# Moving every activation tile of a streamed fp32 matmul chain to one fixed byte distance from the weight tiles

## The chip, the cores and the metric

The kernel runs on one core of one Trainium2 chip. The metric is the device time of one execution in microseconds (us), taken as the median of several executions. Five engines matter: TensorE (PE in the profile, with its weight loads shown apart as PEld), VectorE (DVE), ScalarE (ACT), GpSimd (POOL), and SyncE (SP), which issues all DMAs.

## The reference

Two layers of a decoder trunk on 256 positions of width 1024, batch 1, all in fp32. Layer 0 mixes tokens by dilated window attention, layer 1 by an mLSTM block; each layer then has a squared-ReLU MLP and a gated embedding.

```
for i in range(2):
    if i == 0:
        x = x + dilated_attention(rms_norm(x, a_norm), a_w_qkv, ..., a_w_o)
    else:
        x = x + mlstm_mixer(rms_norm(x, b_norm), b_w_up, ..., b_w_down)
    x = x + squared_relu_mlp(rms_norm(x, mlp_norm[i]), mlp_w1[i], mlp_w2[i])   # 1024 -> 4096 -> 1024
    gate = sigmoid(rms_norm(x, ple_norm[i]) @ ple_w_gate[i])
    x = x + gate * (p[i] @ ple_w_proj[i])
```

Nearly all the arithmetic is in products of 256 positions with large weight matrices: `a_w_qkv` (1024 x 9216), `a_w_o`, `b_w_up` (1024 x 4096), `b_w_down` (2048 x 1024), two pairs `mlp_w1`, `mlp_w2` and two `ple_w_gate`.

## The kernel before

**The weight stream.** All weights lie in DRAM as one sequence of units of 128 partitions x 2048 fp32 (1 MB), in the order of use: `qkv`, `proj0`, `woA`, `woB`, `w1_0`, `w2_0`, `gate0`, `xm`, `z0` to `z3`, `wd0`, `proj1`, `wd1`, `w1_1`, `w2_1`, `gate1`. SyncE fetches a unit four units ahead into one of three `raw` buffers. `split` (lines 180 and 181) turns 512 columns at a time into a rounded part `hi` (ACT) and a remainder `lo` (DVE), both of type fp32r, in 12 rotating buffers each. Each buffer is 2048 bytes long in a partition, so all of them start at the same byte modulo 256.

**The matmuls.** Activations are held the same way, as a pair of high and low part. `stream` (lines 335 to 337) does three matmuls for each 128 x 128 weight tile and adds them up in PSUM:

```
mm(acc[:, q], wh, h, start=first, stop=False, ...)   # L335
mm(acc[:, q], wh, l, start=False, stop=False, ...)   # L336
mm(acc[:, q], wl, h, start=False, stop=last, ...)    # L337
```

Here the weight tile (512 bytes of a partition's row) is the stationary operand and is loaded anew for each matmul; the activations (256 columns, 1024 bytes) are the moving one. In `qkv_block` (lines 503 to 505) it is the other way round: the activations are stationary and 512 columns of weights move.

**Which activations meet the weights.** `hh`/`hl` (the pair `hA`): `qkv`, `w1_0`, `xm`, `z0` to `z3`, `wd1`, `gate1`. `oTh`/`oTl`: `woA`, `woB`. `hidh`/`hidl`: `w2_0`, `w2_1`. `hGh`/`hGl`: `gate0`. `hBh`/`hBl`: `wd0`, `w1_1`. `pT`: `proj0`, `proj1`. `hWh`/`hWl`: two of the 18 blocks of `qkv`.

**What sets the order.** Work is counted in slots of four weight tiles. `at(slot, f)` hangs small pieces of work on a slot, and they are written out when the slot closes, so they stand between stream matmuls on TensorE. Ahead of each `w1`, `gate` and `xm` stretch, `rstd_rows` does so twice: `st.total` (line 276, four short matmuls in the trace) two slots in, and `spread` (line 297, four more) six slots in. In the mLSTM part (`xm` to `wd0`) many more pieces stand between them.

**Where tiles lie.** Pools take SBUF from the low end in the order in which they are opened (or from the high end, with `side="right"`), and tiles follow each other within a pool, so every size moves what comes behind it. Two tiles that nobody uses, `gap0` and `gap1` of 64 bytes, stand ahead of and behind the pools of `hi` and `lo`.

Of the kernel before, what the change touches and what calls it, by code (L numbers as in the profile page):

```python
# [10 lines left out]
F32 = mybir.dt.float32  # L11
F32R = mybir.dt.float32r
I32 = mybir.dt.int32
AF = mybir.ActivationFunctionType
# [4 lines left out]
D, S, P = 1024, 256, 128  # L19
# [113 lines left out]
def build(tc, a):  # L133
    nc = tc.nc
    ctx = ExitStack()
    with ctx:
        _build(ctx, tc, nc, a)


def _build(ctx, tc, nc, a):  # L140
    def pool(n, b=1, c=ctx, **k):
        if "space" not in k:
            k["reuse_waits"] = "tile"
        return c.enter_context(tc.tile_pool(name=n, bufs=b, **k))

    base = pool("base")
# [1 line left out]

    pool("gap0").tile([P, 16], F32, name="gap0")
    hip, lop = pool("hi", 3 * UC // HU), pool("lo", 3 * UC // HU)  # L150
    pool("gap1").tile([P, 16], F32, name="gap1")
    psa = pool("psa", 3, space=PSUM)
    pst = pool("pst", 2, space=PSUM)
    pss = pool("pss", 2, space=PSUM)
# [3 lines left out]
    act = nc.scalar.activation  # L158
# [67 lines left out]


    xctx0 = ExitStack()
    x = pool("x0", c=xctx0, side="right").tile([P, KT, S], F32, name="x")
    prm = base.tile([P, NP], F32, name="prm")  # L230
    ident = base.tile([P, P], F32, name="ident")
    ones = base.tile([P, P], F32, name="ones")
# [6 lines left out]
                nc.sync.dma_start(x[:, 2 * j:2 * j + 2], a["x"][:, 2 * j:2 * j + 2])  # L239
            nc.sync.dma_start(raw[u][:, j * 512:(j + 1) * 512], a["w"][u, :, j * 512:(j + 1) * 512])  # L240
    nc.sync.dma_start(ident, a["eye"])
    first = base.tile([P, 1], F32, name="first")
    act(first, ones[:, 0:1], AF.Exp)

    warm = psm.tile([P, 512], F32, name="sm")
    for _ in range(WARM):
# [5 lines left out]

    hA = [base.tile([P, KT, S], F32R, name=f"h{n}") for n in "hl"]
    sqp = pool("sq", 2)

    class Stats:

# [25 lines left out]
    def rsqrt(y, v, shape):  # L283
        t = sqp.tile(shape, F32, name="rt")
        dve.tensor_scalar(y.bitcast(I32), v.bitcast(I32), -0.5, RSQRT_MAGIC, op0=ALU.mult, op1=ALU.add)
        for _ in range(3):
            dve.tensor_tensor(t, y, y, op=ALU.mult)
            dve.scalar_tensor_tensor(t, t, -0.5, v, op0=ALU.mult, op1=ALU.mult)
            dve.scalar_tensor_tensor(y, t, 1.5, y, op0=ALU.add, op1=ALU.mult)
# [62 lines left out]
    atp = pool("attn", c=actx)  # L352
# [24 lines left out]

    def first_stats():
        st.total()
        sw = atp.tile([P, P], F32, name="sw")  # L380
        dve.tensor_copy(sw[:, 0:64], st.s[:, 192:256])
        dve.tensor_copy(sw[:, 64:128], st.s[:, 0:64])
        for n, t in ((2, st.s[:, 64:192]), (3, sw)):
            mm(st.ps[:, 256 + n:257 + n], t, ones[:, 0:1], start=True, stop=True)
        v = atp.tile([P, 4], F32, name="v4")
        dve.tensor_scalar(v, st.ps[:, 256:260], 1.0 / D, EPS, op0=ALU.mult, op1=ALU.add)
        dve.tensor_scalar(epsx, v[:, 0:2], EPS, None, op0=ALU.mult)
        rsqrt(rx, v, [P, 4])

    def wrap():  # L390
        for n in range(2):
            act(hW[n][:, :, 0:64], hA[n][:, :, 192:256], AF.Copy)
            act(hW[n][:, :, 64:128], hA[n][:, :, 0:64], AF.Copy)

    at(0, first_stats)
    at(8, wrap)

# [281 lines left out]

    mctx = ExitStack()  # L680
    mp = pool("mlp0", c=mctx)
    hid = [mp.tile([P, 32, S], F32R, name=f"hid{n}") for n in "hl"]
    hgp = pool("hG", c=xctx0, side="right")
    hG = [hgp.tile([P, KT, S], F32R, name=f"hG{n}") for n in "hl"]
# [4 lines left out]

    xp1 = pool("x1")  # L690
    xn = xp1.tile([P, KT, S], F32, name="xn")
    hB = [xp1.tile([P, KT, S], F32R, name=f"hB{n}") for n in "hl"]
    mctx = ExitStack()
    mp = pool("gate0", c=mctx)
# [18 lines left out]
    lp = pool("lstm", c=lctx)  # L713
# [123 lines left out]
    def gates_c():  # L837
        ps = SMALL["ps"]
        for b in range(2):
            nc.tensor.transpose(ps[0:4, 16 + b * P:16 + (b + 1) * P], ai[:, b], ident)  # L840
        arow = lp.tile([4, S], F32, name="arow")
        dve.tensor_copy(arow, ps[0:4, 16:16 + S])
        dve.tensor_tensor_scan(Mrow, arow, arow, -3e38, ALU.max, ALU.max)

# [12 lines left out]
    zp = None  # L857
# [94 lines left out]
    for part, _ in CORE:  # L952
        if part == "z0":
            z_units(0, lp)
            while fill:
                for f, args in fill.pop(min(fill)):
                    f(*args)
            close_x()
            t = clock[0]
            for n, f in zip(GT, (gates_b, gates_c, gates_d)):  # L960
                at(t + n, f)
            for h in range(4):
                for n, f in zip(HO, (decay, memory, factor, merge)):
                    at(t + HS[h] + n, f, h)
        elif part[0] == "z":
            z_units(int(part[1]), zp)
        elif part == "proj1":
            prep, ph = proj(1, zp, ("nsq0", "nsq1", "zt"))
            prep()
            stream(B_PROJ, from_h(ph), proj_done)  # L970
        else:
            down(int(part[2]))
# [3 lines left out]
    mp = pool("mlp1", c=mctx)  # L976
# [102 lines left out]
```

## Time and profile before

| | |
|---|---|
| median of 3 executions | 913.3 us (908.6, 913.3, 913.77) |
| profiled execution, its own time | 912.26 us |
| its span from first to last instruction | 910.5 us |
| mean granted TensorE clock | 0.997 |
| PE busy | 894.8 us, 98% of the span, 6924 instructions |
| PEld busy | 833.9 us, 92% |
| DVE busy | 659.2 us, 72% |
| ACT busy | 568.5 us, 62% |
| POOL busy | 39.4 us, 4% |
| DMA queue 1 | 149.12 MB, 47.4% of 16 engines' span |

A matmul's duration in the profile is from its start to its modelled end, and the next one starts long before that; two matmuls of 0.28 us stand about 0.12 us apart. How fast TensorE goes is therefore read from the distance between starts (the **pace**, below), not from the durations. The profiled execution has 1.8 us outside its span.

### The profile page before, as it was taken

How to read it: one execution, taken by the hardware profiler on the slowest of the kernel's cores; microseconds unless marked ns; L12 is line 12 of the kernel's file. 1: busy time of each engine (PE TensorE's matmuls, PEld its weight loads, DVE VectorE, ACT ScalarE, POOL GpSimd, SP SyncE). 2: the span in 40 equal slices, each digit the busy share in tenths (PEclk: the TensorE clock that was granted, in tenths of full speed). 3: DMA queues.
4: the chain of work that ended last, by engine and by line, in shares of the span. 5: the costliest groups of instructions: out<-in, count | busy, mean ns of one | idle time of the engine just before them, and what ended most of it. 6: DMA issues, size and time to landing. Idle time of an engine off the chain costs nothing.

```text
span 910.5 us, 17609 instructions
## 1 busy us (share of the span) xinstructions
PE 894.8 (98%) x6924; PEld 833.9 (92%) x6924; DVE 659.2 (72%) x1409; ACT 568.5 (62%) x1055; POOL 39.4 (4%) x77
## 2 busy tenths in 40 slices
PE   8799999999999999999999999999999999999997
PEld 7687787777889999999999989999999999999997
DVE  6966877857876977765666987668898766656664
ACT  7567576676675766655555777678766666655552
POOL 0410000000000000000000343000000000000000
PEclk9999999999999999999999999999999999999999
DMA  8744434445343455555555433442256555555521
GB/s 305 282 140 147 178 130 150 143 141 180 132 148 137 149 188 185 190 183 188 187 191 175 154 130 134 140 140 93 94 197 223 175 187 188 188 183 188 190 102 47
DMA packets 23122, 150.23 MB, mean 165 GB/s; under 512 B 2560, under 2 KB 3200, under 8 KB 5632
## 3 DMA queue, kind: packets, MB, share of 16 engines
q1 hardware_dynamic: 23040, 149.12, 47.4%
q8 instruction: 54, 0.88, 0.4%
q14 instruction: 28, 0.23, 0.1%
HBM read 148.06 MB, written 1.05 MB: 164 GB/s over the span
## 4 chain that ended last, share of the span: by engine, by line
PE 92%; DVE 6%; issue 1%; ACT 1%; DMA 0%; SPq 0%; ACTq 0%
PE acc L335 21%; PE acc L336 21%; PE acc L337 20%; PE acc L503 6%; PE acc L505 6%; PE acc L504 6%; DVE lo L181 2%; PE tp L455 1%; PE tp L556 1%; PE sm L574 1%; PE sc L531 1%; PE tp L745 1%; PE tp L755 1%; PE sc L886 1%; PE sc L763 1%
## 5 line engine op out<-in xcount | busy, mean ns | idle before, releaser
L181 DVE TENSOR_TENSOR lo<-raw,hi 128x512 fp32r<-128x512 f32 x552 | 375.3, 690 | 169.2 <-ACT hi L180 163.8
L180 ACT ACTIVATE hi<-raw 128x512 fp32r<-128x512 f32 x552 | 338.7, 628 | 216.8 <-PE acc L336 194.1
L335 PE MATMUL acc<-hh,hi 128*128 128x256 f32 x640 | 182.5, 285 | 0.2 <-ACT hh L302 0.2
L336 PE MATMUL acc<-hl,hi 128*128 128x256 f32 x640 | 179.8, 281 | 0.4 <-DVE hl L303 0.3
L337 PE MATMUL acc<-hh,lo 128*128 128x256 f32 x640 | 179.7, 281 | 0.0
L337 PE MATMUL acc<-hidh,lo 128*128 128x256 f32 x512 | 143.3, 280 | 0.0
L336 PE MATMUL acc<-hidl,hi 128*128 128x256 f32 x512 | 143.3, 280 | 0.0
L335 PE MATMUL acc<-hidh,hi 128*128 128x256 f32 x512 | 143.1, 279 | 0.0
L336 PEld LDWEIGHTS acc<-hl,hi 128*128 128x128 f32 x640 | 121.7, 190 | 1.0 <-DVE hl L303 0.8
L335 PEld LDWEIGHTS acc<-hh,hi 128*128 128x128 f32 x640 | 120.7, 189 | 1.5 <-issue 0.7
L337 PEld LDWEIGHTS acc<-hh,lo 128*128 128x128 f32 x640 | 120.3, 188 | 0.0
L503 PE MATMUL acc<-hi,hh 128*128 128x512 f32 x264 | 109.9, 417 | 0.0
L504 PE MATMUL acc<-lo,hh 128*128 128x512 f32 x264 | 104.4, 396 | 0.8 <-DVE lo L181 0.8
L505 PE MATMUL acc<-hi,hl 128*128 128x512 f32 x264 | 104.8, 397 | 0.0
L336 PEld LDWEIGHTS acc<-hidl,hi 128*128 128x128 f32 x512 | 96.3, 188 | 0.0
L335 PEld LDWEIGHTS acc<-hidh,hi 128*128 128x128 f32 x512 | 96.2, 188 | 0.0
L337 PEld LDWEIGHTS acc<-hidh,lo 128*128 128x128 f32 x512 | 96.0, 188 | 0.0
L336 PE MATMUL acc<-hBl,hi 128*128 128x256 f32 x320 | 89.9, 281 | 0.0
L335 PE MATMUL acc<-hBh,hi 128*128 128x256 f32 x320 | 89.8, 281 | 0.0
L337 PE MATMUL acc<-hBh,lo 128*128 128x256 f32 x320 | 89.5, 280 | 0.0
L335 PEld LDWEIGHTS acc<-hBh,hi 128*128 128x128 f32 x320 | 60.3, 188 | 0.3 <-issue 0.3
L336 PEld LDWEIGHTS acc<-hBl,hi 128*128 128x128 f32 x320 | 60.1, 188 | 0.0
(258 smaller groups left out, 1382.7 us busy)
## 6 DMA issues: line engine op xcount, KB each, us to landing
raw<-w SPq DMA_DIRECT2D x136, 1024.0 KB, 4.9
raw<-w SPq DMA_DIRECT2D x8, 256.0 KB, 5.9
x<-x SPq DMA_DIRECT2D x4, 256.0 KB, 5.6
pj<-rep SPq DMA_DIRECT2D x1, 896.0 KB, 6.7
out<-u SPq DMA_DIRECT2D x3, 256.0 KB, 2.4
pT<-p SPq DMA_DIRECT2D x2, 256.0 KB, 3.9
nd<-nd SPq DMA_DIRECT2D x1, 384.0 KB, 5.6
out<-u SPq DMA_DIRECT2D x2, 128.0 KB, 1.9
```

The costliest lines, as they stand in the source:

```text
L180: act(hi[n][:, d], raw[u][:, s], AF.Copy)
L181: dve.tensor_tensor(lo[n][:, d], raw[u][:, s], hi[n][:, d], op=ALU.subtract)
L335: mm(acc[:, q], wh, h, start=first, stop=False, skip_group_check=n > 1)
L336: mm(acc[:, q], wh, l, start=False, stop=False, skip_group_check=n > 1)
L337: mm(acc[:, q], wl, h, start=False, stop=last, skip_group_check=n > 1)
L455: nc.tensor.transpose(ps[:, pair, b * P:(b + 1) * P], n[:, b, ty * 256 + pair * P:ty * 256 + (pair + 1) * P], ident)
L503: mm(accs[b], hh, wh, start=(k == 0), stop=False)
L504: mm(accs[b], hh, wl, start=False, stop=False)
L505: mm(accs[b], hl, wh, start=False, stop=(k == 7))
L531: mm(ps[:, 0:256], q[r, pair, tb], k[r, pair], start=first, stop=last)
L556: nc.tensor.transpose(psf[:, k * P:(k + 1) * P], pe[:, k * P:(k + 1) * P], ident)
L574: mm(out, VT[qt, 0][:, n, cols], pt[:, n * P:(n + 1) * P], start=(n == 0), stop=False, skip_group_check=True)
```

## The change

No operation is added to the stream, and none changes its engine or its place; each engine's instructions stand in the same order. What changes is where tiles lie. `gap1` and the 4-byte tile `first` go, four unused tiles `gapx...` are put in, and two small tiles share the room of others: `sw` that of `t2`, `arow` that of one `w` buffer. The Exp at the start (it makes ACT load its table) now writes two columns of a buffer of the pool `sq`.

```
-    pool("gap1").tile([P, 16], F32, name="gap1")
...
+    pool("gapx4", c=xctx0, side="right").tile([P, 32], F32, name="gapx4")
...
-    first = base.tile([P, 1], F32, name="first")
-    act(first, ones[:, 0:1], AF.Exp)
...
+    act(sqp.tile([P, 2], F32, name="v"), ones[:, 0:2], AF.Exp)
...
-        sw = atp.tile([P, P], F32, name="sw")
+        sw = atp.tile([P, P], F32, name="sw", tag="t2")
...
     mp = pool("mlp0", c=mctx)
+    mp.tile([P, 48], F32, name="gapx1")
     hid = [mp.tile([P, 32, S], F32R, name=f"hid{n}") for n in "hl"]
...
     xn = xp1.tile([P, KT, S], F32, name="xn")
+    xp1.tile([P, 48], F32, name="gapx2")
     hB = [xp1.tile([P, KT, S], F32R, name=f"hB{n}") for n in "hl"]
...
-        arow = lp.tile([4, S], F32, name="arow")
+        arow = zp.tile([4, S], F32, name="arow", tag="w", bufs=2)
```

Addresses in the two built programs, as byte offset modulo 256 (the high and the low part of each pair agree; the last two columns are moving operand minus stationary operand, modulo 256, from -128 to 127):

| tile | before | after | distance before | distance after |
|---|---|---|---|---|
| `hi`, `lo` | 192 | 160 | | |
| `hh`, `hl` in `stream` | 128 | 96 | -64 | -64 |
| `oTh`, `oTl` | 192 | 96 | 0 | -64 |
| `hidh`, `hidl` | 0 | 96 | +64 | -64 |
| `hGh`, `hGl` | 224 | 96 | +32 | -64 |
| `hBh`, `hBl` | 0 | 96 | +64 | -64 |
| `pT` of `proj0` | 224 | 128 | +32 | -32 |
| `pT` of `proj1` | 160 | 0 | -32 | +96 |
| `hh`, `hl` in `qkv_block` (they are stationary) | 128 | 96 | +64 | +64 |
| `hWh`, `hWl` in `qkv_block` | 0 | 160 | -64 | 0 |
| `raw` | 128 | 96 | | |
| `ones` (stationary in line 297) | 96 | 96 | | |
| `dg` (moving in line 297) | 0 | 160 | -96 | +64 |

## Rows read from the trace of the kernel before

**Rows 1.** The page: busy time, and the chain that ended last.
```profile
PE 894.8 (98%) x6924; PEld 833.9 (92%) x6924; DVE 659.2 (72%) x1409; ACT 568.5 (62%) x1055; POOL 39.4 (4%) x77
...
PE 92%; DVE 6%; issue 1%; ACT 1%; DMA 0%; SPq 0%; ACTq 0%
```

**Rows 2.** Matmuls of line 335 by moving tile: count, durations in ns (min/median/max), first and last start.
```profile
L335 PE MATMUL acc<-hh,hi x640: 275/281/470, 303.0 to 905.3; 128*128 128x256 f32 x160
...
L335 PE MATMUL acc<-hidh,hi x512: 278/279/282, 394.6 to 881.9; 128*128 128x256 f32 x171
...
L335 PE MATMUL acc<-hBh,hi x320: 278/279/388, 643.5 to 791.5; 128*128 128x256 f32 x160
...
L335 PE MATMUL acc<-oTh,hi x64: 278/284/385, 270.6 to 302.6; 128*128 128x256 f32 x64
...
L335 PE MATMUL acc<-hGh,hi x64: 277/280/364, 485.0 to 508.1; 128*128 128x256 f32 x64
```

**Rows 3.** Timeline of PE: first matmul of `w1_0`, `w2_0`, `gate0`, `w1_1`, `w2_1`, `gate1`.
```profile
302.98 0.36 PE L335 MATMUL acc<-hh,hi 128*128 128x256 f32 x1
...
394.56 0.28 PE L335 MATMUL acc<-hidh,hi 128*128 128x256 f32 x1
...
485.02 0.28 PE L335 MATMUL acc<-hGh,hi 128*128 128x256 f32 x1
...
700.46 0.28 PE L335 MATMUL acc<-hBh,hi 128*128 128x256 f32 x1
...
791.81 0.28 PE L335 MATMUL acc<-hidh,hi 128*128 128x256 f32 x1
...
882.26 0.28 PE L335 MATMUL acc<-hh,hi 128*128 128x256 f32 x1
```

**Rows 4.** Timeline of PE in `woB`: two starts, 23 matmuls apart.
```profile
300.07 0.28 PE L335 MATMUL acc<-oTh,hi 128*128 128x256 f32 x1
...
302.83 0.28 PE L337 MATMUL acc<-oTh,lo 128*128 128x256 f32 x1
```

**Rows 5.** Timeline of PE in `xm`: two starts, 11 matmuls apart.
```profile
562.83 0.28 PE L335 MATMUL acc<-hh,hi 128*128 128x256 f32 x1
...
564.07 0.28 PE L337 MATMUL acc<-hh,lo 128*128 128x256 f32 x1
```

**Rows 6.** Timeline of PE in `w1_0` behind lines 276 and 297 (11 starts each).
```profile
309.44 0.28 PE L336 MATMUL acc<-hl,hi 128*128 128x256 f32 x1
...
310.61 0.28 PE L337 MATMUL acc<-hh,lo 128*128 128x256 f32 x1
...
314.12 0.28 PE L336 MATMUL acc<-hl,hi 128*128 128x256 f32 x1
...
315.30 0.28 PE L337 MATMUL acc<-hh,lo 128*128 128x256 f32 x1
```

**Rows 7.** Timeline of PE in `gate1` ahead of and behind line 276.
```profile
882.84 0.28 PE L337 MATMUL acc<-hh,lo 128*128 128x256 f32 x1
...
883.97 0.28 PE L335 MATMUL acc<-hh,hi 128*128 128x256 f32 x1
...
886.92 0.28 PE L336 MATMUL acc<-hl,hi 128*128 128x256 f32 x1
...
888.10 0.28 PE L337 MATMUL acc<-hh,lo 128*128 128x256 f32 x1
```

**Rows 8.** Groups by line, DVE: the split, and line 303 on three tiles.
```profile
L181 DVE TENSOR_TENSOR lo<-raw,hi 128x512 fp32r<-128x512 f32 x552 | 375.3, 690 | 169.2 <-ACT hi L180 163.8
...
L303 DVE SCALAR_TENSOR_TENSOR hl<-xn,prm,hh 128x256 fp32r<-128x256 f32 x16 | 7.5, 481 | 0.0
...
L303 DVE SCALAR_TENSOR_TENSOR hGl<-x,prm,hGh 128x256 fp32r<-128x256 f32 x8 | 3.9, 485 | 0.0
```

**Rows 9.** Timeline: ACT's first work behind the Exp, and the copy into `arow`.
```profile
5.05 0.91 ACT L302 ACTIVATE hh<-x,prm 128x256 fp32r<-128x256 f32 x2 [2.83 <-DMA x<-x]
...
605.24 0.41 DVE L842 COPY arow<-sm 4x256 f32<-4x256 f32 x1 [0.34 <-PE sm L840]
```

## The prediction

> **What bounds the kernel now.** I read the page first, then the groups by line, then TensorE's timeline. TensorE is busy 98% of the span and has 92% of the chain that ended last, DMA 0% [rows 1]. So the time is the number of matmuls times their pace, plus a few waits near the start, and a change of addresses can only matter here through the pace. The timeline shows three paces for one and the same loop (lines 335 to 337), all at a granted clock of 1.00:
>
> - 120.0 ns for `oT`, at distance 0: 302.83 - 300.07 = 2.76 us for 23 matmuls [rows 4].
> - 117.8 ns for `hid`, at +64: `w2_0` takes 485.02 - 394.56 = 90.46 us for its 768 matmuls, `w2_1` 882.26 - 791.81 = 90.45 us, both without a break [rows 3].
> - For `hh`, at -64, both 113 and 118 ns. In `xm` 1.24 us for 11 matmuls, 112.7 ns [rows 5]; at the start of `gate1` 1.13 us for 10, 113 ns [rows 7]. But behind the short matmuls of line 276 in the same `gate1` it is 1.18 us for 10, 118 ns [rows 7], and in `w1_0` it is 117 and 118 ns behind lines 276 and 297 [rows 6]; the whole of `w1_0` takes 394.56 - 302.98 = 91.58 us [rows 3], which is 768 x 117.8 = 90.5 us and 1.1 us for the breaks.
>
> The exact steps are 113.3, 117.8 and 120.0 ns as far as these rows resolve them (340 ns for three matmuls, 353 and 360). The durations say the same: line 335 with `hh` goes down to 275 ns, with `hid` and `hB` (+64) never below 278, with `oT` its median is 284 [rows 2]. So the fast pace is seen at -64 and, in the stretches quoted at 0 and +64, not there. But -64 alone does not bring it: the pace is taken up when a stretch begins or a break ends, and then held, in `w2_0` for all 768 matmuls.
>
> **What the change moves.** 192 matmuls with `oT`, 1536 with `hid`, 192 with `hG` and 960 with `hB` (three lines by the counts of [rows 2]) come to -64: 2880 in all. The 1920 with `hh` keep their distance, and so does nearly all of `qkv`.
>
> *What I take as certain.* `oT` loses its 120.0: 192 x 2.2 = 0.4 us if it takes 117.8, 192 x 6.7 = 1.3 us at 113.3. `hG` needs 508.1 - 485.0 = 23.1 us [rows 2] from its first to its 190th matmul with two breaks on the way; 189 x 117.8 ns are 22.3 us, and the breaks take some 0.7, for `w1_0` spends 1.1 on its own; so 0.1 us is won, and 0.8 more at 113.3. `wd0` (`hB`, 192 matmuls, between pieces of the mLSTM) is the stretch most like `xm`, where the fast pace comes and goes; I give it half of 192 x 4.4 = 0.8 us, so 0.4. Against it stand the matmuls of `gate1` ahead of line 276, some 35 between 882.84 and 886.92 [rows 7], which are fast now after coming over from +64; without that step in distance they may stay at 117.8, 0.2 us lost.
>
> *What decides.* Four long stretches hang together in two pairs, `w1_0` with `w2_0` and `w1_1` with `w2_1`, since `hid` now lies as the tile ahead of it and the pace is held across the change of tile. Each of the four is worth 768 x 4.4 = 3.4 us between 117.8 and 113.3, a pair 6.8. The pace of a pair is set by the last break ahead of it, line 297 in the seventh slot of `w1`. In the rows at -64 such sums end in 118 ns three times out of three [rows 6, 7]. So I take the pairs at 117.8: nothing is won there. This is the term I know least: between 0 and 13.6 us, and no row excludes either end. What speaks for a change even here is that `dg` moves from -96 to +64 against `ones`, so that the break itself ends differently.
>
> *Small edits.* The Exp on two columns lies in ACT's idle time of 2.83 us ahead of the first `hh`, which waits for a DMA [rows 9]. The copy into `arow` (0.41 us [rows 9]) now also waits for POOL's last reader of that room, which built matrices for `xm`, a stretch long past; if it did wait, the exponentials of the first head would be late, not the stream. Both 0. The two `hW` blocks, 96 matmuls of 512 columns, go to a distance not seen there; between one step of 6.7 ns less and one more (the step between 113.3 and 120.0), +-0.6 us, taken as 0. `pT`, 96 matmuls, also +-0.6, taken as 0. The other engines read and write at new addresses too: line 303 takes 481 ns into a tile at 128 and 485 into one at 224 modulo 256 [rows 8], so I price that at 0; and the split, 0.69 us for four weight tiles on DVE [rows 8], stays far under TensorE's 12 x 113.3 = 1.36 us, so nothing else becomes the bound if TensorE speeds up.
>
> *The sum.* -0.4 - 0.1 - 0.4 + 0.2 = -0.7 us on the profiled execution's 912.26: 911.5 us. That execution lies 1.0 us under the median of 913.3; the three runs spread over 5 us (908.6 to 913.8), which is about what one long stretch would give if it took up the other pace.
>
> *A rule against this.* The rows give `oT` 120.0 ns and `hh` 112.7 with the same loop at two distances [rows 4, 5]. The Trainium skill, page "TensorE: Matmul & The Clock Gate", section "Part 2: What happens when you issue a matmul", says that TensorE has two independent SBUF read ports and that loading the next weights takes no read bandwidth from the running matmul. By that rule the distance is worth nothing and the time stays at 912.3; the trace does not agree, since two paces 6 to 7 ns apart stand there at equal clock and without waits.
>
> **The rivals.**
>
> *All long stretches go fast* (chance 0.26). If the new break ends in the pace of [rows 5], it does so in both pairs, for all addresses in it agree. For: the fast pace is held for 35 matmuls of `gate1` without a slip until the break, and behind many breaks of `xm`. Against: three sums out of three. Moved matmuls alone: 1.3 + 3.4 x 3 (`w2_0`, `w1_1`, `w2_1`) + 0.9 + 0.8 = 13.2 us, 899 us; with `w1_0` and some of `wd1` and `gate1`, up to 5 us more, 894. I say 897.
>
> *One pair goes fast* (0.22). The two pairs come to their breaks from unlike stretches, `w1_0` from `woB` and `w1_1` from `wd1`, and spend unlike times on them, 1.1 us and 791.81 - 700.46 - 90.5 = 0.9 us [rows 3]; in `gate1` a break turned the pace round [rows 7]. 912.3 - 6.8 - 0.8 = 904.7 us.
>
> *Slower* (0.10). Weights and activations now both start 32 bytes off a multiple of 64, where before the weights never did. If rows are read in pieces of 64 bytes, each matmul's 1024 bytes and each weight row's 512 touch one piece more, and the pace could become 120.0 everywhere. 2880 - 192 + 1920 - 768 = 3840 matmuls would go from 117.8 to 120.0, 8.5 us, and the 768 of `xm` and `z0` to `z3` (16 units of 16 tiles) lose between 768 x 2.2 = 1.7 and 768 x 6.7 = 5.1 us: 922.5 to 926, say 924. It decides from the point where `w2_0` takes more than 90.5 us. Against: `hG` starts at 224, 32 off, and its durations have a median of 280 ns like the others [rows 2]; that the weights are off as well is not in the trace.
>
> **How the numbers follow.** Pace unchanged in the long stretches, 911.5 us (own range 909 to 915, the upper end from the median and highest run of before): 0.42. Range: the cases from "all fast" to this one hold 0.90; 896.5 to 915 leaves out the slower case and a tail of "all fast". The median before is 913.3, and 1% of it, about what a measurement of this kernel tells from no change, is 9.1 us: faster means under 904.2. Faster: 0.26, and 0.07 of the 0.22 of "one pair": 0.33. Slower by over 1%: above 922.4, 0.09. Within: 0.58.
>
> **What would show it.** In the profile after, the time from the first `hid` to the first `hG` matmul tells the case: 90.5 us as now, 87.0 if fast, 92.2 if slow; likewise for `w2_1`. Line 335 with `hid` would show a minimum of 275 to 277 ns instead of 278. `oT` must leave 120.0 ns (2.76 us for 23 matmuls), or distance modulo 256 is not what sets the pace. `qkv`, up to `proj0` at 262 us, should stay within 1 us. I am wrong if `hid` and `hB` show a pace that `hh` never had, or if the time moves where no stream matmul stands.

## The result and the profile after

The changed kernel takes 904.74 us (median of 6 executions, 904.17 to 905.53), the kernel before 910.0 us on the same chip (6 executions, 908.6 to 913.77): a ratio of 0.9925, 95% interval 0.9907 to 0.9944. The time lies in the predicted range, but not by the case taken as likeliest. It is the rival "one pair goes fast", worked out at 904.7 us, that came about. One execution each of experiments 4 and 5 took over 4900 us, and one of the kernel before on the chip of experiments 7 and 8 took 1038.56 us; these three are left out of all figures below.

The profiled execution after took 905.53 us. The page of it, busy times and the chain that ended last:

```profile
PE 887.6 (98%) x6924; PEld 825.9 (91%) x6924; DVE 659.1 (73%) x1409; ACT 568.7 (63%) x1055; POOL 38.7 (4%) x77
...
PE 91%; DVE 6%; issue 1%; ACT 1%; DMA 1%; SPq 0%; ACTq 0%; DVEq 0%
```

Nothing but TensorE has changed against [rows 1]: the same 6924 instructions, 7.2 us less busy time, and DVE, ACT and POOL within 0.7 us. TensorE still has nearly the whole chain.

Line numbers are one lower than before: the stream is lines 334 to 336, the sums are line 275 and `spread` is line 296. Line 334 by moving tile, as in [rows 2]:

```profile
L334 PE MATMUL acc<-hidh,hi x512: 276/278/281, 392.0 to 875.1; 128*128 128x256 f32 x171
...
L334 PE MATMUL acc<-oTh,hi x64: 276/276/384, 271.9 to 303.0; 128*128 128x256 f32 x64
```

`oT` has left its slow pace: its median goes from 284 to 276 ns. `hid` shows a minimum of 276 where it had 278, so some of its matmuls run at the fast pace; which, the starts tell. The timeline of PE after, the first matmul of `w1_0`, `w2_0`, `gate0`, `wd1`, `w1_1`, `w2_1` and `gate1` (`wd1` has no row in [rows 3]; before, it began at 677.85):

```profile
303.57 0.36 PE L334 MATMUL acc<-hh,hi 128*128 128x256 f32 x1
...
391.97 0.28 PE L334 MATMUL acc<-hidh,hi 128*128 128x256 f32 x1
...
479.01 0.28 PE L334 MATMUL acc<-hGh,hi 128*128 128x256 f32 x1
...
672.01 0.28 PE L334 MATMUL acc<-hh,hi 128*128 128x256 f32 x1
...
693.77 0.28 PE L334 MATMUL acc<-hBh,hi 128*128 128x256 f32 x1
...
784.96 0.28 PE L334 MATMUL acc<-hidh,hi 128*128 128x256 f32 x1
...
875.41 0.28 PE L334 MATMUL acc<-hh,hi 128*128 128x256 f32 x1
```

Each stretch is the difference of two neighbours, set against [rows 2, 3]:

| stretch | before, us | after, us | difference |
|---|---|---|---|
| up to the first `oT` matmul | 270.6 | 271.9 | +1.3 |
| `oT` | 32.4 | 31.7 | -0.7 |
| `w1_0` | 91.58 | 88.40 | -3.2 |
| `w2_0` | 90.46 | 87.04 | -3.4 |
| `gate0` to the end of `wd0` and `proj1` | 192.83 | 193.00 | +0.2 |
| `wd1` | 22.61 | 21.76 | -0.85 |
| `w1_1` | 91.35 | 91.19 | -0.2 |
| `w2_1` | 90.45 | 90.45 | 0 |
| `gate1` and the end | 28.2 | 28.3 | +0.1 |

The sum is -6.7 us, the difference of the two spans (910.45 and 903.75). The first line is no effect to explain: the first `oT` matmul stood anywhere from 270.4 to 272.3 us in the profiled executions of the experiments below. Nearly all of the gain is one pair of stretches at 113.3 ns a matmul. The other pair, at the same distance of -64, stayed at 117.8.

Where the two pairs part is seen at the breaks. The timeline of PE after, in `w1_0` ahead of the sums (line 275), at them, and behind `spread` (line 296); then in `w1_1` ahead of the sums and behind them:

```profile
308.00 0.28 PE L335 MATMUL acc<-hl,hi 128*128 128x256 f32 x1
...
309.18 0.28 PE L336 MATMUL acc<-hh,lo 128*128 128x256 f32 x1
309.34 0.61 PE L275 MATMUL sm<-ones,ssum 128*128 128x1 f32 x4
...
314.56 0.28 PE L335 MATMUL acc<-hl,hi 128*128 128x256 f32 x1
...
315.69 0.28 PE L336 MATMUL acc<-hh,lo 128*128 128x256 f32 x1
...
696.60 0.28 PE L335 MATMUL acc<-hBl,hi 128*128 128x256 f32 x1
...
697.73 0.28 PE L336 MATMUL acc<-hBh,lo 128*128 128x256 f32 x1
697.85 0.50 PE L275 MATMUL sm<-ones,ssum 128*128 128x1 f32 x4
...
698.41 0.28 PE L335 MATMUL acc<-hBl,hi 128*128 128x256 f32 x1
...
699.59 0.28 PE L336 MATMUL acc<-hBh,lo 128*128 128x256 f32 x1
```

Behind line 296 in `w1_0` ten steps take 1.13 us: 113 ns. Behind line 275 in `w1_1` they take 1.18 us: 118 ns. There are two visible differences between the breaks. The first is a wait: in `w1_0` the sums start 0.16 us behind the matmul ahead of them, because DVE has only just written their operand `ssum`; in `w1_1` they start after 0.12 us, an ordinary step. Call the first a break with a wait and the second a break without one. The second difference is the pace that the break finds: `w1_0` came to its sums at 118 ns (1.18 us for ten steps) and left them faster, `w1_1` came at 113 (1.13 us) and left them slower.

### The profile page after: what moved, and what is told of

Its sections match the earlier page's. It is cut to its first block, busy times and chain, and to the rows that moved or that the text cites. A ratio compares the mean times of both kernels' runs of the same rounds, so it can differ in the third digit from the quotient of the medians.

```text
span 903.7 us, 17611 instructions
## 1 busy us (share of the span) xinstructions
PE 887.6 (98%) x6924; PEld 825.9 (91%) x6924; DVE 659.1 (73%) x1409; ACT 568.7 (63%) x1055; POOL 38.7 (4%) x77
## 4 chain that ended last, share of the span: by engine, by line
PE 91%; DVE 6%; issue 1%; ACT 1%; DMA 1%; SPq 0%; ACTq 0%; DVEq 0%
PE acc L334 20%; PE acc L335 20%; PE acc L336 20%; PE acc L502 6%; PE acc L504 6%; PE acc L503 6%; DVE lo L180 2%; PE tp L454 1%; PE tp L555 1%; PE sm L573 1%; PE sc L530 1%; PE tp L746 1%; PE tp L756 1%; PE sc L887 1%; PE sc L764 1%
## 5 line engine op out<-in xcount | busy, mean ns | idle before, releaser
L336 PEld LDWEIGHTS acc<-hBh,lo 128*128 128x128 f32 x320 | 61.3, 192 | 0.0
L504 PEld LDWEIGHTS acc<-hi,hl 128*128 128x128 f32 x264 | 50.1, 190 | 11.5
```

The lines of the kernel that those rows point to most:

```text
L336: mm(acc[:, q], wl, h, start=False, stop=last, skip_group_check=n > 1)
L504: mm(accs[b], hl, wh, start=False, stop=(k == 7))
```

## The experiments

**What was to be told apart.** The theory behind the prediction: distance modulo 256 says which paces are possible, a break picks one, and it is held until the next break. Three things were open. Did `hid`'s own address bring the gain? Is 113.3 possible at all distances, so that only breaks matter? And what in a break picks the pace: the form of its instructions, its time, or where its operands lie? All ratios are to the kernel before on the same chip. Line numbers shift by a few between kernels; the stream, the sums and `spread` are recognized by their tiles.

**1. The layer-0 `hid` put back to +64** (changed kernel):

```
-    mp.tile([P, 48], F32, name="gapx1")
+    mp.tile([P, 80], F32, name="gapx1")
```

> The changed kernel with one tile pair put back: hid of layer 0 lies at +64 again (192 bytes of unused room become 320), all else at -64. Theory (the distance modulo 256 limits which paces a stretch can have, a break picks one, and it is held until the next break or change of distance): w1_0 stays at 113.3 ns, w2_0 goes from 87.0 to 90.5 us, 768 x 4.4 ns = 3.4 us more, so 908.1 us against 904.7 of the changed kernel. Rival (the distance is beside the point; what helps layer 0 is some other shift, such as all tiles 32 bytes off a multiple of 64, or the moved small tiles): w2_0 stays at 87.0 us and the time at 904.7.

Measured: 909.21 us (10 executions, 907.67 to 911.82), ratio 0.9996 [0.9985, 1.0006]. The gain of the change is gone. The timeline of PE in its profiled execution (911.82 us, the longest of the ten), ahead of the sums in `w1_0` and at them, and at both ends of `w2_0`:

```profile
307.23 0.28 PE L335 MATMUL acc<-hl,hi 128*128 128x256 f32 x1
...
308.36 0.28 PE L336 MATMUL acc<-hh,lo 128*128 128x256 f32 x1
308.71 0.61 PE L275 MATMUL sm<-ones,ssum 128*128 128x1 f32 x4
...
394.51 0.28 PE L334 MATMUL acc<-hidh,hi 128*128 128x256 f32 x1
...
484.96 0.28 PE L334 MATMUL acc<-hGh,hi 128*128 128x256 f32 x1
```

At +64 `w2_0` takes 90.45 us, as before. But here `w1_0`, which came to the sums at 113 ns (1.13 us for ten steps), left them at 118, with the same instructions at the same addresses that went from 118 to 113 in the profile after. The wait ahead of the sums was longer, 0.35 us instead of 0.16. So `w1_0` takes different ways through the same break from execution to execution, and this run alone doesn't tell what `hid` would have done behind a fast `w1_0`. Experiments 9 and 10 tell it: each has a place where matmuls at +64 follow matmuls at -64 that went at 113 ns, and there they went at 118 (36 matmuls of `hB` behind `wd1`, 24 of the copy in `w1_0`). No `w1` or `w2` stretch at +64 was fast in any profile.

**2. Only `hid` moved to -64, in both layers** (kernel before):

```
     mp = pool("mlp0", c=mctx)
+    mp.tile([P, 32], F32, name="gaph")
     hid = [mp.tile([P, 32, S], F32R, name=f"hid{n}") for n in "hl"]
... (the same line ahead of layer 1's hid)
```

> The kernel before with one part of the change alone: hid of both layers moved from +64 to -64 by 128 bytes of unused room ahead of it. Theory: w2_0 follows w1_0, which is at 117.8 ns and -64, so it inherits 117.8: 90.5 us as before. w2_1 follows w1_1 at +64, a step in distance like the one into gate1, behind which the pace was 113 ns: 87.0 us, 3.4 us less, so 906.6 us against 910.0. Rival 1 (-64 alone brings 113.3): both w2 stretches take 87.0 us, 903.2 us in all. Rival 2 (the step into -64 does nothing for a long stretch): 910 us.

Measured: 902.53 us (901.65 to 903.22), ratio 0.9918 [0.9902, 0.9935]: at least as good as the whole change, whose interval overlaps with it. The timeline of PE, the ends of `w2_0` and of `w2_1`:

```profile
392.43 0.28 PE L335 MATMUL acc<-hidh,hi 128*128 128x256 f32 x1
...
479.47 0.28 PE L335 MATMUL acc<-hGh,hi 128*128 128x256 f32 x1
...
786.23 0.28 PE L335 MATMUL acc<-hidh,hi 128*128 128x256 f32 x1
...
873.27 0.28 PE L335 MATMUL acc<-hh,hi 128*128 128x256 f32 x1
```

Both take 87.04 us. The second is the surprise: `w1_1` ahead of it ran at 117.8 with `hB` at +64, and the pace turned at the first `hid` matmul, with no break between. A step of the moving tile from +64 to -64 does what a break can do. `gate1` before, fast for its first matmuls after coming over from +64 [rows 7], had shown the same in small. So `hid` at -64 is the part that pays, and moving `hB` as well took this step away from `w2_1`.

**3. All stream tiles at distance 0.** In the changed kernel `gap0` goes and `gap1` comes back, so that `hi` and `lo` lie 64 bytes lower and everything else stays:

```
-    pool("gap0").tile([P, 16], F32, name="gap0")
...
+    pool("gap1").tile([P, 16], F32, name="gap1")
```

> The changed kernel with hi and lo 64 bytes lower and every other tile where it was: the distance is 0 for hh, oT, hid, hG and hB. Theory (120.0 ns belongs to distance 0): w2_0 and w2_1 take 768 x 120.0 = 92.2 us each, against 87.0 and 90.5; w1_0 and w2_0 lose 10.2 us, w1_1 and w2_1 3.4, the rest about 6: 924 us. Rival (the distance is beside the point): 905 us, the two w2 stretches as in the changed kernel.

Measured: 923.5 us (922.5 to 924.51), ratio 1.0152 [1.0137, 1.0167]. The timeline of PE, the ends of `w2_0`:

```profile
396.58 0.28 PE L334 MATMUL acc<-hidh,hi 128*128 128x256 f32 x1
...
488.74 0.28 PE L334 MATMUL acc<-hGh,hi 128*128 128x256 f32 x1
```

92.16 us for 768 matmuls, 120.0 ns each, and the same in `w2_1`. At this distance no break brought 113 ns or held 118. The distance does matter by itself.

**4. The sums over 128 columns.** In `w1_1` a break of one-column products had turned the fast pace down. Here (changed kernel) the sums of line 275 write 128 equal columns instead of one (`w` is 128):

```
-                mm(self.ps[:, 256 + b:257 + b], self.s[:, b * P:(b + 1) * P], ones[:, 0:1], start=True, stop=True)
+                c = 256 + b * w
+                mm(self.ps[:, c:c + w], self.s[:, b * P:(b + 1) * P], ones[:, 0:w], start=True, stop=True)
...
```

> The changed kernel with the sums of the five later norms made over 128 equal columns of ones instead of one column: the two products of line 275 get the shape of the two of line 296, behind which each stretch of the changed kernel kept the pace that it had. Theory (the one-column products are what turns 113.3 into 117.8 in gate0 and w1_1): w1_1, w2_1, gate0 and gate1 take 113.3 ns nearly throughout; w2_1 goes from 90.5 to 87.0 us, w1_1 from 91.1 to about 88, the gates lose 0.5 each; about 8 us less than the changed kernel, 897 us. Rival (any break without a wait ends in 117.8, or layer 1 is slow for its addresses): 904.7 us, w2_1 at 90.5.

Measured: 906.28 us (4 executions, 905.64 to 906.64), ratio 0.996 [0.9946, 0.9974]. Not faster than the change, so the form of the product is not the reason. One more execution of the same kernel, for its timeline:

> The kernel with sums over 128 columns of ones once more, for its trace. Its time was 906.5 us, 1.7 over the changed kernel, so the theory that one-column products are what turns 113.3 into 117.8 has no support from the time. What is left: either w2_1 is at 90.5 us and the form of the product does not matter, or w2_1 is at 87.0 and w2_0 lost the same in exchange (90.5 instead of 87.0).

Measured: 904.91 us. The timeline of PE in `w1_1`, at the wide sums and behind them:

```profile
697.25 0.61 PE L276 MATMUL sm<-ones,ssum 128*128 128x128 f32 x4
...
697.81 0.28 PE L337 MATMUL acc<-hBl,hi 128*128 128x256 f32 x1
...
698.99 0.28 PE L338 MATMUL acc<-hBh,lo 128*128 128x256 f32 x1
```

1.18 us for ten steps: still 118 ns behind the break, now with 128 columns (the row says 128x128).

**5. The breaks of `w1` two slots later** (changed kernel; those of the gates and of `xm` stay). On TensorE the sums come behind 60 matmuls, in `w1_0` instead of 48, in `w1_1` instead of 36:

```
-        at(clock[0] + SA, st.total)
-        at(clock[0] + SB, finish)
+        late = 2 if power == 2 else 0
+        at(clock[0] + SA + late, st.total)
+        at(clock[0] + SB + late, finish)
```

> The changed kernel with the two breaks of w1_0 and w1_1 (lines 275 and 296) two slots later, so that the one-column products of w1_0 no longer wait for DVE's sum of squares. Theory (one-column products that come without a wait leave 117.8 ns behind at -64; those of w1_0 leave 113.3 in most executions because TensorE waited there): w1_0 falls to 117.8 behind the break and w2_0 inherits it, 90.5 us instead of 87.0: 6.5 us more than the changed kernel, 911 us. Rival (w1_0 is fast for its addresses or for what comes ahead of it): w2_0 stays at 87.0 us and the time at 904.7.

Measured: median 911.18 us (9 executions), in two groups, three from 904.6 to 906.1 and six from 911.0 to 912.7; ratio 0.9996 [0.9969, 1.0022]. The timeline of PE in `w1_0` of the profiled execution (912.14 us):

```profile
310.40 0.28 PE L337 MATMUL acc<-hh,lo 128*128 128x256 f32 x1
310.51 0.50 PE L275 MATMUL sm<-ones,ssum 128*128 128x1 f32 x4
...
311.07 0.28 PE L336 MATMUL acc<-hl,hi 128*128 128x256 f32 x1
...
312.25 0.28 PE L337 MATMUL acc<-hh,lo 128*128 128x256 f32 x1
```

With the wait gone (0.11 us to the sums), `w1_0` behaves like `w1_1`: fast ahead of the sums, 1.18 us for ten steps behind them, and `w2_0` inherits that with 90.45 us. The wait is not all that differs from the profile after, where `w1_0` came to its sums at 118 ns. The two groups lie 6.5 us apart, about one pair of stretches; as `ssum` was ready 1.2 us ahead of the sums here, a wait for it hardly parts them. No execution of the shorter group was profiled, so what does stays open.

**6. All stream tiles 32 bytes higher.** The prediction's slower rival blamed starts that are 32 bytes off a multiple of 64. Here (changed kernel) they are on one, with every distance in the stream kept:

```
-    pool("gapx4", c=xctx0, side="right").tile([P, 32], F32, name="gapx4")
+    pool("gapx4", c=xctx0, side="right").tile([P, 24], F32, name="gapx4")
...
+    base.tile([P, 8], F32, name="gaps")
     hA = [base.tile([P, KT, S], F32R, name=f"h{n}") for n in "hl"]
```

> The changed kernel with 32 bytes of unused room ahead of hh, so that weights and activations start at 192 and 128 modulo 256, multiples of 64, at the same distance of -64. Theory (only the distance counts): 904.7 us within 1 us, w1_0 and w2_0 at 113.3 ns, w1_1 and w2_1 at 117.8 behind their breaks, as in the changed kernel. Rival (starting 32 bytes off a multiple of 64 matters, for better or worse): all stream matmuls go to another pace, 3840 x 2.2 ns = 8 us or more to either side.

Measured: 899.03 us (898.01, 898.71, 899.35, 903.96), ratio 0.9897 [0.9856, 0.9938]; the expected value was missed by 5.7 us, for the better. The timeline of PE in `w1_1` behind `spread`:

```profile
704.07 0.28 PE L336 MATMUL acc<-hBl,hi 128*128 128x256 f32 x1
...
705.20 0.28 PE L337 MATMUL acc<-hBh,lo 128*128 128x256 f32 x1
```

The sums had left 118 ns here as well, but `spread` now turns it to 113 (1.13 us for ten). `w1_1` takes 88.16 us and `w2_1` 87.04. Either 64-byte starts help, or the small operands of the break: `dg` moved with the rest, from 160 to 192, while `ones` stayed at 96. One of the four executions, 903.96 us, did not have the gain.

**7. Only `ones` moved, from 96 to 64** (changed kernel; 224 bytes ahead and 32 behind, so everything later moves by 256 bytes and keeps its place modulo 256):

```
+    base.tile([P, 56], F32, name="gapo")
     ones = base.tile([P, P], F32, name="ones")
...
+    base.tile([P, 8], F32, name="gapp")
```

> The changed kernel with the tile ones alone at another place modulo 256: 64 instead of 96 (224 bytes of unused room ahead of it and 32 behind it, so that all later tiles move by 256). Stream tiles stay at 160 and 96, 32 off a multiple of 64. In the kernel with all stream tiles 32 bytes higher, line 297 (296 here) turned 117.8 into 113.3 each time; there ones lay 96 bytes behind hi and lo, here it does too, against 64 in the changed kernel. Theory (only distances count, those of the operands in the break included): the same turn here, w1_1 and w2_1 at 113.3 ns behind line 296, gates too: 899 us. Rival (that kernel was faster because rows of the stream start at multiples of 64 bytes): 904.7 us, w2_1 at 90.5 us.

Measured: 898.05 us (897.75 to 898.44), before on that chip 913.2, ratio 0.983 [0.9815, 0.9846]: the fastest kernel of the study. The timeline of PE behind the sums and behind `spread` in `w1_1`, and the ends of `w2_1`:

```profile
698.40 0.28 PE L337 MATMUL acc<-hBl,hi 128*128 128x256 f32 x1
...
699.57 0.28 PE L338 MATMUL acc<-hBh,lo 128*128 128x256 f32 x1
...
704.50 0.28 PE L337 MATMUL acc<-hBl,hi 128*128 128x256 f32 x1
...
705.64 0.28 PE L338 MATMUL acc<-hBh,lo 128*128 128x256 f32 x1
...
781.91 0.28 PE L336 MATMUL acc<-hidh,hi 128*128 128x256 f32 x1
...
868.95 0.28 PE L336 MATMUL acc<-hh,hi 128*128 128x256 f32 x1
```

1.17 us for ten steps behind the sums, 1.14 behind `spread`, 87.04 us for `w2_1`. No tile of the stream has moved modulo 256, and they start 32 bytes off a multiple of 64 as in the change. So 64-byte starts are out, and a tile of ones that is read in breaks of 0.5 us decides over a pair of 180 us.

**8. Experiment 6 with `dg` put back to 0** (where the kernel before had it; unused tiles of 64 and 192 bytes around it in its pool):

```
+            sqp.tile([P, 16], F32, name="gapd", bufs=1)
...
+            sqp.tile([P, 48], F32, name="gape", bufs=1)
```

> The kernel with all stream tiles 32 bytes higher (899 us), with one tile moved: dg, the moving operand of line 297, from 192 to 0 modulo 256 (64 bytes of room ahead, 192 behind), where it lay in the kernel before: +64 against hi and lo instead of 0. Theory (ones and dg decide together how the break ends): line 297 keeps the pace again that it finds, as in the kernel before and the changed kernel: w1_1 and w2_1 at 117.8 ns, 904 to 905 us. Rival (ones alone decides): 899 us, w2_1 at 87.0.

Measured: 905.05 us (6 executions, 903.64 to 910.03), ratio 0.992 [0.9897, 0.9943]. The timeline of PE in `w1_1` behind `spread`, and in `gate1` behind the sums:

```profile
703.30 0.28 PE L343 MATMUL acc<-hBl,hi 128*128 128x256 f32 x1
...
704.47 0.28 PE L344 MATMUL acc<-hBh,lo 128*128 128x256 f32 x1
...
879.00 0.28 PE L343 MATMUL acc<-hl,hi 128*128 128x256 f32 x1
...
880.14 0.28 PE L344 MATMUL acc<-hh,lo 128*128 128x256 f32 x1
```

1.17 us again, and `w1_1` and `w2_1` take 91.19 and 90.45 us where experiment 6 had 88.16 and 87.04: with only `dg` moved, the second pair is slow again. (The whole times of experiments 6 and 8 are from two chips, on which the kernel before takes 909.87 and 913.2 us.) In `gate1` the sums, without a wait, turned 118 ns into 113 (1.14 us for ten steps), while at the same addresses in experiment 6 they turned 113 into 118. So what the sums leave also depends on the pace that they find.

**9. `hB` put back to +64** (changed kernel), which gives `w2_1` its step again:

```
-    xp1.tile([P, 48], F32, name="gapx2")
+    xp1.tile([P, 80], F32, name="gapx2")
     hB = [xp1.tile([P, KT, S], F32R, name=f"hB{n}") for n in "hl"]
+    xp1.tile([P, 32], F32, name="gapx3")
```

> The changed kernel with hB alone put back to +64 (128 bytes of unused room moved from behind it to ahead of it). Theory: w1_1 keeps 117.8 ns, which its breaks left in the changed kernel as well, and the step from +64 to -64 at the start of w2_1 brings 113.3: w2_1 takes 87.0 us instead of 90.5, wd0 loses up to 0.3, so 901.5 us. Rival 1 (hB at -64 is worth what it looks): 904.7 us or more. Rival 2 (the step does nothing): 904.7, w2_1 at 90.5.

Measured: 901.8 us (10 executions: seven from 901.2 to 902.7, and 904.33, 909.66, 909.66), ratio 0.9929 [0.9903, 0.9954]. The timeline of PE, the ends of `w2_1`:

```profile
784.75 0.28 PE L334 MATMUL acc<-hidh,hi 128*128 128x256 f32 x1
...
871.79 0.28 PE L334 MATMUL acc<-hh,hi 128*128 128x256 f32 x1
```

87.04 us: the step works again, in a second kernel. In `w1_0` this execution took a third way: the sums, which start 0.17 us behind the matmul ahead of them, left 118 ns, and `spread` turned it to 113. The change, experiment 1 and this kernel have the same addresses up to the end of `w1_0`.

**10. An artificial step inside `w1`** (changed kernel). Weight tiles 33 to 40 of each `w1` read a copy of four pieces of the normed activations that lies at +64, in room of `hid` that is still free:

```
+            h = tmp_h if 32 <= i < 40 else h1
+            return h[0][:, k], h[1][:, k]
...
+        at(clock[0] + 3, fill_step)
```

> The changed kernel with a step in distance made on purpose in each w1, behind its breaks: four 256-column pieces of the normed activations are computed a second time (8 small ACT and 8 small DVE instructions in each w1) into room of hid at +64, and 8 of the 512 weight tiles, from the 33rd on, read that copy; from the 41st on the tiles at -64 are read again. Theory (a step from +64 to -64 brings 113.3 ns, whatever the break left): w1_0 and w2_0 are at 113.3 in every execution, and now w1_1 behind tile 40 and w2_1 too: w2_1 87.0 us instead of 90.5 and w1_1 about 88 instead of 91, 6.5 us less than the changed kernel: 898 us. Rival 1 (the step works only when the tile changes for good): 904.7. Rival 2 (the second computation delays the split of the weights): 906 or more, with TensorE waiting for hi or lo at the start of w1.

Measured: 905.67 us (904.31 to 906.11), ratio 0.9945 [0.9927, 0.9963]: nothing won over the change. The timeline of PE in `w1_1`, behind `spread` and so ahead of the copy, and behind the copy:

```profile
705.11 0.28 PE L335 MATMUL acc<-hBl,hi 128*128 128x256 f32 x1
...
706.28 0.28 PE L336 MATMUL acc<-hBh,lo 128*128 128x256 f32 x1
...
709.35 0.28 PE L335 MATMUL acc<-hBl,hi 128*128 128x256 f32 x1
...
710.52 0.28 PE L336 MATMUL acc<-hBh,lo 128*128 128x256 f32 x1
```

In `w1_1` the pace was 118 ns ahead of the copy, on it and behind it, and `w2_1` took 90.45 us. In `w1_0` it was 113 ahead of the copy, 118 on it and 113 again behind it: the step gave back what the copy had taken. So a step from +64 to -64 is no sure means either.

**11. Experiment 7 with the sums' operand moved**, `ssum` from 224 to 96, by taking a neighbour's small buffer ahead of it:

```
+            if not gaps:
+                gaps.append(sqp.tile([P, 2, 8], F32, name="rt"))
```

> The kernel with ones at 64 (898 us), with ssum, the stationary operand of the four short products that come two slots into each w1, gate and xm, moved by 128 modulo 256 (two neighbours of the pool change places): from +64 to -64 against hi and lo. So far these products, when TensorE does not wait ahead of them, left 117.8 ns behind whatever they found; line 298 then turns it into 113.3 four slots later. Theory (the distances of a break's operands decide how it ends): the pace behind the short products may change; if it becomes 113.3, gate0, w1_1 and gate1 each win 47 x 4.4 ns = 0.2 us, and w1_0 as much in the executions that now lose it: 897.4 us. Rival (one-column products always end in 117.8, as the wide ones did): no change, 898 us.

Measured: 904.23 us (903.95 to 905.25), ratio 0.9939 [0.9923, 0.9956]; both expectations missed. The timeline of PE in `gate1` behind the sums:

```profile
879.59 0.28 PE L341 MATMUL acc<-hl,hi 128*128 128x256 f32 x1
...
880.72 0.28 PE L342 MATMUL acc<-hh,lo 128*128 128x256 f32 x1
```

In `gate1` the sums turned 118 into 113 (1.13 us for ten steps), as they did in experiment 8 with `ssum` unmoved, and in `gate0` and `w1_1` they turned 113 into 118, as in experiment 7. What is new is `spread`: its operands lie as in experiment 7, and it found 118 as there, yet it now left `w1_1` at 118, so `w2_1` took 90.45 us. So moving `ssum` changed something in the stream that the pace of 118 does not show. The section on the prediction, under "Open", says what it is.

## Why the prediction came out as it did

**What bounds the kernel** held: apart from the first line, the table above moved by the pace of the stream. Distance 0 gives 120.0 ns (experiment 3); `hid` at +64 gave 117.8, and at -64 both 113.3 and 117.8. That the pace is held, across tiles and for 768 matmuls without a break, held too.

**The step that failed** is "In the rows at -64 such sums end in 118 ns three times out of three", from which follows "So I take the pairs at 117.8". Three sums were taken for a law. In `w1_0`, where TensorE waits ahead of the sums, the break left 113.3 in the profile after, at an unchanged distance, and -3.2 us there became -6.6 because `w2_0`, now at -64, inherits the pace. That this is the address of `hid` is shown by experiment 2 (87.04 us with it moved and everything else left) and by the matmuls at +64 that went at 118 ns directly behind matmuls at 113 (experiments 9 and 10). The way that `w1_0` takes changes between executions (experiments 1, 5 and 9); in the change it was favourable six times out of six, as far as the times from 904.17 to 905.53 tell. In `w1_1`, where no wait stands ahead of the sums, the step was right: 118 ns, nothing won. The rival "one pair goes fast" named this cause, that the two pairs come to their breaks from unlike stretches, and its 904.7 us. That the stated range was met says little about the mechanism: from 896.5 to 915 us it held three of the four cases.

**The smaller terms.** `oT`: 0.4 to 1.3 us forecast, 0.7 measured. `hG`: 0.1 forecast, 23.47 to 23.35 us measured, 0.1, but by luck: before, at +32, it did not run at 117.8 throughout, as the prediction had it. Its first 36 matmuls took 120.0 ns and its last 108 took 116.7, a pace that the prediction's list of three lacks. `wd0` was oversized: half of its matmuls were to go fast, 14 of the 186 steps between neighbours did. The miss was made up by `wd1`, which keeps its distance and was not counted; it won 0.85 us because the pace that it starts with, behind the products with `pT`, is now 113.3; in experiment 2, where `pT` had not moved, `wd1` kept 117.8. Which of the moved tiles does it was not tried apart. `gate1` did lose its fast start, as said; its fast matmuls had come from the step that the change removes. The small edits and the other engines cost nothing that shows.

**"Slower"** is out: at -64 no stretch was seen at a pace above 117.8, and experiment 7 reached 898.05 us with starts 32 bytes off a multiple of 64.

**"All long stretches fast"** at 897 us was not what the change did, but its size was right: with `ones` moved the second pair goes fast and the time is 898.05 us. What stood in the way was not the stream's distance but the operands of the breaks. The prediction had named this possibility ("the break itself ends differently").

**The rule against this.** The same 768 matmuls take 87.04 us at distance -64 and 92.16 at 0. The Trainium skill, page "TensorE: Matmul & The Clock Gate", section "Part 2: What happens when you issue a matmul", has loading the next weights take nothing from the running matmul's reads. By that the two would be equal; the measurement decides against it for these operands.

**Two sizes for one gain.** The profiled executions differ by 6.7 us, the medians by 5.3. The profiled execution before (912.26 us) is one of the kernel's longer ones; in its shorter ones `w1_0` may already have run at 113.3 behind its wait, as it did in experiment 2 with the same sums at the same addresses. That is argued, not shown: no shorter execution of it was profiled.

**Open** is the mechanism that maps operand addresses, and the state a stream comes with, to the pace behind a break or a step. But the state itself can be read. The trace gives starts to 1 ns. At 113.3 the three steps of a weight tile are alike to that 1 ns; at 117.8, averaged over a stretch, one takes 118.3 ns and two take 117.5. The longer step is behind the first of the three matmuls in some stretches (call it variant A: `w2_1` before), behind the second in others (B: `w2_1` in experiment 8) or behind the third (C: `w2_1` in the change). Sorted by this, the breaks without a wait are regular. Each field says what a break leaves when it finds the stream at 113 ns or at 118 in variant A, B or C:

| break, stream at -64 | finds 113 | finds A | finds B | finds C |
|---|---|---|---|---|
| sums, `ssum` at +64 to the weights | C | | 113 | C |
| sums, `ssum` at -64 (experiment 11) | B | | 113 | |
| `spread` in the change | 113 | 113 | | C |
| `spread` in experiments 6, 7 and 11 | 113 | 113 | B | 113 |
| `spread` before and in experiments 2 and 8 | 113 | | B | B |

The twelve profiles with a stream at -64 hold 76 such breaks (the sums and `spread` of `w1` and the gates, at this distance), and none leaves anything else than its field says; the fields with A or B, and the second row, rest on one or two breaks each, the others on three or more. The sums over 128 columns of experiment 4 are in the first row. This explains experiment 11: the sums there left B instead of C, and `spread`, which turns C into 113, leaves B as it is. Steps from +64 to -64 fit too: A became 113 in four of four (`gate1` before, experiments 2 and 9, `w1_0` in experiment 10), and C stayed C in two of two (`w1_1` in experiment 10, `gate0` in experiment 1). The table was read from the runs after they were made; it has not been used to forecast one, and the breaks with a wait are not in it.

## What to carry to other kernels

In a TensorE-bound stream that loads a weight tile for every matmul, read the distance between matmul starts stretch by stretch: one loop can run at several paces with no wait in sight, and the addresses of moving and stationary operand modulo 256 are worth varying. A few tiny matmuls between two stretches can set the pace of the next 1450, so their operands' addresses deserve the same care as the stream's. What a break leaves depends on the state that it finds, so try several placements on the chip, profile more than one execution, and read the steps of one weight tile apart before you call two stretches alike; reasoning from three breaks to the next was not enough here.

## What the runs showed of the hardware that was not expected

- The paces at distances 0 and -64 are 120.0 ns and 113.3 or 117.8 ns a matmul, at a granted clock of 0.996. In `w2_1` of the change, at 117.8, each of the 767 steps took 117 to 119 ns: it is a pace of its own, and no mixture of steps of 113 and 120.
- Two paces are stable at one and the same set of addresses: behind `spread`, `w1_0` ran 684 matmuls at 117.8 ns in experiment 1 and at 113.3 in the change, and `w2_1` at -64 ran all its 768 at 117.8 in the change (90.45 us) and at 113.3 in experiment 7 (87.04 us).
- A change of the moving tile alone, with no other instruction between, can switch the pace (`w2_1` in experiments 2 and 9).
- `w1_0`, whose first matmul starts 0.38 us late and whose sums wait too, went three ways in three executions with the same addresses (the change, experiments 1 and 9). That the waits are what makes executions differ is not shown; the times of experiment 5, without a wait at the sums, still lie in two groups 6.5 us apart.
